# The opening of a hybrid encoder layer: raw x loaded into places of later operands, sums two tiles behind, first outputs inside the first pair

## The chip, the cores and the metric

The kernel runs on one core of a Trainium2 chip. The metric is the time of one execution on the device, in microseconds (us). The engines are PE (TensorE, matrix products), DVE (VectorE), ACT (ScalarE), POOL (GpSimd) and SP (SyncE); here SP's queue issues every DMA. All engines run on their own and wait for each other through semaphores. Each works through its own queue strictly in order, so an instruction that waits holds up all behind it.

## What is computed

The reference is one layer of an encoder: an RMS norm of x (1280 tokens of 2048 channels, 1024 of one sequence and 256 of another), one large projection to 9232 columns, 2-D neighbourhood attention on a part of them, a bidirectional mLSTM on another part, gates, an output projection with the residual, and a last RMS norm.

```python
hn = rmsnorm(x, norm_w)
proj = jnp.einsum('btd,dp->btp', hn, w_in)
...
mixed = jnp.concatenate([att, mem], axis=-1)
return x + jnp.einsum('btm,md->btd', mixed, w_out)
```

Everything is fp32. Only the beginning of the projection matters here.

## The kernel before, in words

**Precision.** A product of fp32 matrices is made from two-part operands: a high part (a cast to fp32r, on ACT) and a low part (the rest, on DVE). Three matmuls replace one: high by high, high by low, low by high (`mm_c`, L186). `split_a` (L157) writes such a pair of parts; `split` (L149) does the same with a scale.

**Stage A of the projection.** The first 768 tokens (GA; two halves of HALF = 384) are projected for all columns, in pairs of 128-column tiles. A pair (`pair_a`, L316) is done in seven products instead of eight: the channels (two halves f of 1024, each of 8 tiles kk) and the tokens (two halves c) form a 2 x 2 block of x, and sums and differences of the blocks are operands of the products. `xop(i, kk, b)` gives operand i: `xb11[kk]` is the upper left block, `xg[0..2, kk]` hold the lower row (products 2 and 3), and two made of sums (6 and 5, 4 and 7). All are kept in SBUF for the whole of stage A. The norm's factor of each token is not applied to x but to the outputs, once it is known.

**The opening.** `first_tiles` (L196) makes these operands and, while that goes on, already computes the first four column tiles in the plain way, with eight accumulators `fb`, one in each PSUM bank. Its loop over kk (0 to 7) does this:
- loads raw x of the tiles kk and kk + 8 (`x_raw`, L107, names `xr`) into buffers of the tag "pc" (NPC = 5 of them), and weights `fr` (L204) into one of NRA = 3 buffers of the tag "ra";
- scales both raw x by the norm's weight (L221, ACT), splits the weights into four `fw` tiles (tag "wsa", NWS = 8), the upper left block into `xb`, the upper right one into `fx` (tag "pc") and the lower row into `xg[0]`;
- 48 matmuls (L188): 24 with the upper row (h = 0) and 24 with the lower row (h = 1);
- four subtractions and additions in place (L241 to L245, DVE), then splits of the results into `xg[1]` and `xg[2]`;
- from kk = 4 on, a load of rows of x (`xq`, L114, tag "ra") and the sum of their squares (`x_square`, L110, ACT).

Eight more squares follow the loop, then the banks are copied out to `fo` (L257 DVE, L259 ACT; tag "pc"), the factor is made of the squares (`x_rstd` L117: a reduction on DVE, L102 and L103 on POOL), spread over the partitions by two small products with six diagonal blocks `xdg` (`x_stats` L123, L131, L134 `rsps`, L135), and the four outputs are scaled by it (`out_scaled`, L161) and written (L265).

**The pairs.** Then come the pairs of the list `order` (L434): A4, A6, A24, A56 and so on; between A6 and A24 stands a small product for the gates (L411). A pair has four stages r, each with one load of 512 KB of weights (L353, tag "ra"), sums of weights on POOL (L358), seven splits (ACT, DVE) and 42 matmuls; in the last stage the products are folded from PSUM into the output tiles `Cn` (tag "pc"). Between products, `next(bg, None)` lets a generator do a piece of background work; after the first pair this is the finishing of the pair before. For the first pair it is empty.

**What sets the order.** The program is not executed in the order of the text. A scheduler orders the instructions of each engine when the kernel is built, and picks for each tile a free buffer of its tag; a load into a buffer waits for the last reader of what lay there. The DMAs also carry eight semaphores in turn, so a DMA waits for the eighth before it.

Of the kernel before, what the change touches and what calls it, by code (L numbers as in the profile page):

```python
# [8 lines left out]
F32 = mybir.dt.float32  # L9
# [21 lines left out]
KC0 = (0, 8, 24, 32)  # L31
BKIND = (0, 1, 1, 2)
BIAS_S = 6 * NAK
XFIRST = (0, 1, 8, 9, 2, 3, 10, 11, 4, 5)
QT0, KT0, GT0, QK0, OT0, ZT0 = 0, 8, 16, 24, 40, 48

# [2 lines left out]
def kernel(  # L39
# [26 lines left out]
    def bank(tag, name):  # L66
        return ps.tile([P, 512], F32, tag=tag, name=name, bufs=3 if tag == "pr" else 5)
# [37 lines left out]
    def x_raw(pool, shape, tag, bufs, g, k):  # L105
        raw = pool.tile([P, shape], F32, tag=tag, name=f"xr{g}_{k}", bufs=bufs)[:, : GSZ[g]]
        DM.dma_start(raw, xT[:, k, GOF[g] : GOF[g] + GSZ[g]])  # L107
        return raw

    def x_square(g, i):  # L110
        t, q = divmod(i, 2)
        r0 = GOF[g] + t * P
        raw = wa.tile([P, 1024], F32, tag="ra", name=f"xq{g}_{i}", bufs=NRA)
        DM.dma_start(raw, xtok[r0 : r0 + P, q * 1024 : (q + 1) * 1024])  # L114
        S.activation(raw, raw, AF.Square, accum_out=ssq[g][:, t, q : q + 1])
# [41 lines left out]
    def split_a(hi, lo, src):  # L157
        S.copy(hi, src)  # L158
        V.tensor_tensor(lo, src, f(hi), op=ALU.subtract)
# [36 lines left out]
    def first_tiles():  # L196
        names = ("pr", "pr", "pr", "a", "a", "a", "a", "a")
        pb = [bank(t, f"fb{j}")[:, :HALF] for j, t in enumerate(names)]
        for kk in range(8):
            wr = wa.tile([P, 1024], F32, tag="ra", name=f"fr{kk}", bufs=NRA)  # L200
            wv = wr.rearrange("p (g j f c) -> p g j f c", g=2, j=2, f=2)
            sc = [x_raw(wa, GA, "pc", NPC, 0, kk)]
# [7 lines left out]
            sc.append(x_raw(wa, GA, "pc", NPC, 0, kk + 8))  # L210
            ws = {}

            def wsplit(h):
                for g_ in range(2):
                    t = wsa(f"fw{kk}_{h}{g_}")
                    hi, lo = (t[:, z].rearrange("p (j c) -> p j c", j=2) for z in range(2))
                    split_a(hi, lo, wv[:, g_, :, h, :])
                    ws[h, g_] = t

            for h in range(2):  # L220
                S.mul(sc[h], sc[h], lnw_sb[:, kk + 8 * h : kk + 8 * h + 1])  # L221
            b11, b12 = sc[0][:, :HALF], sc[0][:, HALF:]
            wsplit(0)
            split_a(xb11[kk][:, 0], xb11[kk][:, 1], b11)
            t12 = wa.tile([P, 2, HALF], F32R, tag="pc", name=f"fx{kk}", bufs=NPC)
            split_a(t12[:, 0], t12[:, 1], b12)
            wsplit(1)
            g0 = xg[0, kk].rearrange("p h c t -> p h (c t)")
            split_a(g0[:, 0], g0[:, 1], sc[1])
            xs = {  # L230
                (0, 0): lambda b_: xb11[kk][:, b_], (0, 1): lambda b_: t12[:, b_],
                (1, 0): lambda b_: xop(2, kk, b_), (1, 1): lambda b_: xop(3, kk, b_),
            }
            for h in range(2):
                for j in range(8):
                    n, c = j // 2, j % 2
                    mm_c(
                        pb[j], lambda a_: ws[h, n // 2][:, a_, (n % 2) * P : (n % 2 + 1) * P],
                        xs[h, c], kk == 0 and h == 0, kk == 7 and h == 1,
                    )  # L240
            V.tensor_tensor(sc[1], sc[1], sc[0], op=ALU.subtract)  # L241
            V.tensor_tensor(b12, b12, b11, op=ALU.subtract)
            d1, t3 = sc[1][:, :HALF], sc[1][:, HALF:]
            V.tensor_tensor(b11, t3, b11, op=ALU.add)
            V.tensor_tensor(d1, d1, t3, op=ALU.subtract)  # L245
            for g_, src in ((1, sc[0]), (2, sc[1])):
                gv = xg[g_, kk].rearrange("p h c t -> p h (c t)")
                split_a(gv[:, 0], gv[:, 1], src)
# [67 lines left out]
    def pair_a(n1, bg=iter(()), hook=None):  # L316
        nm = f"A{n1}"
        tags = ("pr", "pr", "pr", "a", "a", "a", "a")
        order = (1, 5, 6, 4, 7, 2, 3)
        bk = {i: bank(t, f"{nm}b{i}")[:, :HALF] for i, t in zip(order, tags)}  # L320
        Cn = [pc(f"{nm}c{j}") for j in range(2)]
        C = [Cn[q // 2][:, (q % 2) * HALF : (q % 2 + 1) * HALF] for q in range(4)]

        def scaled(q):
            out_scaled(C[q], C[q], rbs[0][:, (q % 2) * HALF : (q % 2 + 1) * HALF], n1)

        def plus(q, src, i):
            V.tensor_tensor(C[q], C[src], bk[i], op=ALU.add)

        def fold(i):  # L330
            if i == 1:
                S.copy(C[0], bk[1])
            elif i == 6:
                plus(1, 0, 6)
            elif i == 7:
                plus(2, 1, 7)
                plus(3, 2, 5)
                plus(1, 1, 5)
                plus(2, 2, 4)
                scaled(3)  # L340
                scaled(2)
            elif i == 2:
                plus(0, 0, 2)
                scaled(0)
            elif i == 3:
                plus(1, 1, 3)
                scaled(1)

        for r in range(4):
            if r == 2 and hook is not None:  # L350
                hook()
            raw = wa.tile([P, 1024], F32, tag="ra", name=f"{nm}r{r}", bufs=NRA)
            DM.dma_start(raw, w_in[n1 // 2, r])  # L353
            A = {(j, f_): raw[:, (2 * j + f_) * 256 :][:, :256] for j in range(2) for f_ in range(2)}

            def summed(i, x, y_, op):
                t = wa.tile([P, 256], F32, tag="wt", name=f"{nm}t{r}{i}", bufs=NWT)
                G.tensor_tensor(t, x, y_, op=op)  # L358
                return t

            src = {1: A[0, 0], 4: A[1, 1], 2: A[0, 1]}
            for i in order:
                if i == 5:
# [15 lines left out]
                if r == 3:  # L379
                    fold(i)  # L380
                elif i in (5, 4, 2):
                    next(bg, None)
        for _ in bg:
            pass
        return finish_a(n1, Cn)
# [1083 lines left out]
```

## Time and profile before

| | us |
|---|---|
| Median of 3 runs (lowest, highest) | 2594.48 (2594.1, 2597.23) |
| The profiled execution | 2593.92 |
| Its span in the profile | 2592.2 |
| PE busy | 2566.7 (99%) |
| DVE busy | 1913.0 (74%) |
| ACT busy | 1310.7 (51%) |
| POOL busy | 559.4 (22%) |

The profile is one execution. Times in its rows are counted from the start of the span. A row of the timeline has start, duration, engine, line, operation, output and input tiles with their form, the number of instructions, and in brackets the idle time before it and what ended that. Two instructions in a row on an engine overlap a little, so that the sum of durations can exceed the time they take together. A row of the waits has the engine, what it was to run, what it waited for, then the sum, the count and the longest. A row of the grouped view has the operation with its form and count, then the sum of the durations and the mean of one in ns, then idle time before them. Matmul records have modelled ends; starts are the better measure.

### The profile page before, as it was taken

How to read it: one execution, taken by the hardware profiler on the slowest of the kernel's cores; microseconds unless marked ns; L12 is line 12 of the kernel's file. 1: busy time of each engine (PE TensorE's matmuls, PEld its weight loads, DVE VectorE, ACT ScalarE, POOL GpSimd, SP SyncE). 2: the span in 40 equal slices, each digit the busy share in tenths (PEclk: the TensorE clock that was granted, in tenths of full speed). 3: DMA queues.
4: the chain of work that ended last, by engine and by line, in shares of the span. 5: the costliest groups of instructions: out<-in, count | busy, mean ns of one | idle time of the engine just before them, and what ended most of it. 6: DMA issues, size and time to landing. Idle time of an engine off the chain costs nothing.

```text
span 2592.2 us, 42374 instructions
## 1 busy us (share of the span) xinstructions
PE 2566.7 (99%) x14470; PEld 2361.1 (91%) x14470; DVE 1913.0 (74%) x3838; ACT 1310.7 (51%) x2988; POOL 559.4 (22%) x857
## 2 busy tenths in 40 slices
PE   8999999999999999999999999999999999999998
PEld 8999999999999999988989989989888888888886
DVE  7858778897878788875487577668567644879695
ACT  7534444444444444543576566567566522335445
POOL 0434444454444444300011010001011000000001
PEclk9999999999999999999999999999999999999999
DMA  6423343333323232445555655655655567646327
GB/s 208 157 78 118 102 135 106 98 102 107 93 96 100 90 116 84 152 127 162 171 171 183 194 155 181 200 169 180 191 183 172 161 231 248 214 127 209 95 86 252
DMA packets 215648, 389.10 MB, mean 150 GB/s; under 512 B 26976, under 2 KB 116232, under 8 KB 215432
## 3 DMA queue, kind: packets, MB, share of 16 engines
q1 hardware_dynamic: 215432, 386.40, 46.7%
q8 instruction: 114, 1.87, 0.3%
q14 instruction: 102, 0.84, 0.1%
HBM read 314.94 MB, written 71.38 MB: 149 GB/s over the span
## 4 chain that ended last, share of the span: by engine, by line
PE 90%; DMA 4%; DVE 2%; ACT 2%; SPq 1%; issue 1%; POOL 0%; ACTq 0%; POOLq 0%; DVEq 0%
PE pc L499 23%; PE po L1303 12%; PE pv L580 6%; PE A24b L188 1%; PE A8b L188 1%; PE A44b L188 1%; PE A40b L188 1%; PE A52b L188 1%; PE A48b L188 1%; PE A20b L188 1%; PE A16b L188 1%; PE A12b L188 1%; PE A54b L188 1%; PE A70b L188 1%; PE A50b L188 1%; PE A68b L188 1%
## 5 line engine op out<-in xcount | busy, mean ns | idle before, releaser
L1303 PE MATMUL po<-wo,mo 128*128 128x512 f32 x1620 | 375.6, 393 | 0.2 <-DVE y L1253 0.2
L1303 PEld LDWEIGHTS po<-wo,mo 128*128 128x128 f32 x1620 | 304.0, 188 | 71.1 <-DVE y L1253 0.7
L152 DVE TENSOR_TENSOR ws<-wr,ws 128x512 fp32r<-128x512 f32 x224 | 152.3, 696 | 96.3 <-ACT ws L151 94.9
L151 ACT CAST ws<-wr 128x512 fp32r<-128x512 f32 x224 | 135.8, 619 | 146.5 <-PE pc L499 101.5
L102 POOL TENSOR_SCALAR rs<-rs 128x1 f32<-128x1 f32 x10 | 3.4, 340 | 541.8 <-DVE rs L1283 541.8
L151 ACT CAST mo<-mb 128x640 fp32r<-128x640 f32 x72 | 51.9, 726 | 108.1 <-PE po L1303 93.6
L152 DVE TENSOR_TENSOR mo<-mb,mo 128x640 fp32r<-128x640 f32 x72 | 58.7, 822 | 33.7 <-ACT mo L151 33.6
L1253 DVE TENSOR_TENSOR y<-y,po 128x512 f32<-128x512 f32 x90 | 58.3, 683 | 9.7 <-PE po L1303 9.4
L152 DVE TENSOR_TENSOR wsv<-wr_v,wsv 128x512 fp32r<-128x512 f32 x64 | 43.6, 690 | 22.1 <-ACT wsv L151 21.8
L151 ACT CAST mo<-ms 128x640 fp32r<-128x640 f32 x40 | 28.9, 726 | 59.9 <-PE po L1303 34.0
L151 ACT CAST wsv<-wr_v 128x512 fp32r<-128x512 f32 x64 | 39.2, 617 | 38.8 <-PE pc L499 23.3
L165 DVE TENSOR_TENSOR pco<-pc,rstdb 128x512 f32<-128x512 f32 x48 | 32.7, 687 | 32.0 <-PE pc L499 29.9
L102 POOL TENSOR_SCALAR mls_0r<-mls_0r 128x2 f32<-128x2 f32 x4 | 0.9, 236 | 245.6 <-ACT mls_0jk L1089 245.6
L274 DVE SCALAR_TENSOR_TENSOR pcv<-pco,cw_sb,pcv 128x516 f32<-128x516 f32 x64 | 46.7, 744 | 0.0
L1266 ACT ACTIVATE jk<-y 128x512 f32<-128x512 f32 x40 | 25.2, 630 | 35.2 <-DVE y L1253 35.0
L152 DVE TENSOR_TENSOR mo<-ms,mo 128x640 fp32r<-128x640 f32 x40 | 32.7, 821 | 7.5 <-ACT mo L151 7.5
L188 PE MATMUL fb<-xg,fw 128*128 128x384 f32 x192 | 35.0, 335 | 1.7 <-ACT xg L158 1.7
L499 PE MATMUL pc<-x_2h,ws 128*128 128x512 f32 x112 | 35.3, 398 | 0.0
L499 PE MATMUL pc<-x_0h,ws 128*128 128x512 f32 x112 | 35.2, 398 | 0.0
L188 PEld LDWEIGHTS fb<-xg,fw 128*128 128x128 f32 x192 | 33.4, 188 | 2.0 <-ACT xg L158 2.0
L499 PE MATMUL pc<-x_1h,ws 128*128 128x512 f32 x112 | 34.5, 395 | 0.0
L499 PE MATMUL pc<-x_8h,ws 128*128 128x512 f32 x112 | 33.9, 396 | 0.0
(1687 smaller groups left out, 8147.9 us busy)
## 6 DMA issues: line engine op xcount, KB each, us to landing
wr<-in_w_in_dram SPq DMA_DIRECT2D x112, 512.0 KB
wr_v<-in_w_in_dram SPq DMA_DIRECT2D x32, 512.0 KB
wb<-in_w_o_dram SPq DMA_DIRECT2D x48, 256.0 KB
xq<-in_xtok_dram SPq DMA_DIRECT2D x20, 512.0 KB
mb<-mx SPq DMA_DIRECT2D x32, 320.0 KB
y<-in_xtok_dram SPq DMA_DIRECT2D x40, 256.0 KB
wr_wp<-in_w_o_dram SPq DMA_DIRECT2D x16, 512.0 KB
xr<-in_xT_dram SPq DMA_DIRECT2D x16, 384.0 KB
```

Of the source, the lines that this page charges most:

```text
L102: G.tensor_scalar(out, ssum, 1.0 / count, EPS, op0=ALU.mult, op1=ALU.add)
L151: S.copy(hi, src)
L152: V.tensor_tensor(lo, src, f(hi), op=ALU.subtract)
L165: V.tensor_tensor(o, src, rb, op=ALU.mult)
L188: PE.matmul(o, w(a_), x(b_), start=first and m == 0, stop=last and m == 2)
L274: V.scalar_tensor_tensor(dst[:, a:n], src[:, a + j - pad : n + j - pad], cw_sb[:, ct, j : j + 1], dst[:, a:n], op0=ALU.mult, op1=ALU.add,)
L499: PE.matmul(pb[j], t[j][:, wi, c : c + P], xs[xi], start=first and m == 0, stop=last and m == 2,)
L580: PE.matmul(outs[tt], xs[:, tt * P : (tt + 1) * P], t[:, wi, q * w : (q + 1) * w], start=first and m == 0 and (gates or tt % 2 == 0), stop ...
L1253: V.tensor_tensor(Y[p, q, tt], Y[p, q, tt], bk, op=op)
L1266: S.activation(jk, Y[p, q, tt], AF.Square, accum_out=ss[t][:, c : c + 1])
L1303: PE.matmul(bk[tt], m[xi][:, tt * P : (tt + 1) * P], w[wi], start=first and kk == 0 and j == 0, stop=last and j == 2, skip_group_check=True,)
```

## The change

- Raw x of kk 0 to 6 no longer goes into the tag "pc". It is loaded into the place of an operand that is made only later: kk 0 to 3 into that of `xg[2, kk + 4]`, kk 4 to 6 into that of `xg[1, kk + 1]`. The operands of `xg` are allocated when first used. Raw x of kk 7 stays in "pc".
- For kk 0 raw x of each half comes in two loads of 384 columns, the first split is made straight from the unscaled raw x (scaling inside the cast and the subtraction), and the products of its 24 matmuls are taken in another order. A multiply of one column of `mhalf` by 1.0 is put ahead of everything on ACT.
- The sums and the splits of the two operands made of them (`sums`) come LAG = 2 channel tiles later. Those of kk 6 and 7, eight of the twelve squares, the factor and the first outputs leave `first_tiles`, which becomes a generator, and are the background work of the first pair.
- In every pair the output tiles `Cn` are taken at stage 3 instead of at the start.

```diff
+LAG = 2
...
+        def ops(g_, kk):
+            if (g_, kk) not in xg:
+                xg[g_, kk] = xa.tile([P, 2, 2, HALF], F32R, tag=f"xg{g_}_{kk}", name=f"xg{g_}_{kk}")
+            return xg[g_, kk]
...
+        def load(kk, h):
+            if kk == 7:
+                r = pc(f"xr{kk}_{h}")
+            elif h == 0:
+                tag = f"xg2_{kk + 4}" if kk < 4 else f"xg1_{kk + 1}"
+                t = xa.tile([P, 2, GA], F32, tag=tag, name=f"xr{kk}")
+                r, raw[kk, 1] = t[:, 0], t[:, 1]
+            else:
+                r = raw[kk, 1]
+            raw[kk, h] = r
+            n = GA if kk else HALF
+            for c in range(0, GA, n):
+                DM.dma_start(r[:, c : c + n], xT[:, kk + 8 * h, c : c + n])
+
+        def scale(kk, h):
+            r = raw[kk, h]
+            n = GA if kk else HALF
+            for c in range(0, GA, n):
+                S.mul(r[:, c : c + n], r[:, c : c + n], lnw_sb[:, kk + 8 * h : kk + 8 * h + 1])
+
+        def sums(kk):
+            r0, r1 = raw[kk, 0], raw[kk, 1]
+            V.tensor_tensor(r1, r1, r0, op=ALU.subtract)
+            V.tensor_tensor(r0[:, HALF:], r0[:, HALF:], r0[:, :HALF], op=ALU.subtract)
+            V.tensor_tensor(r0[:, :HALF], r1[:, HALF:], r0[:, :HALF], op=ALU.add)
+            V.tensor_tensor(r1[:, :HALF], r1[:, :HALF], r1[:, HALF:], op=ALU.subtract)
+            for h in range(2):
+                split_a(slot(1 + h, kk, 0), slot(1 + h, kk, 1), raw[kk, h])
+
+        S.mul(mhalf[:, 15:16], ones[:, 0:1], 1.0)
         for kk in range(8):
...
-            for h in range(2):
-                S.mul(sc[h], sc[h], lnw_sb[:, kk + 8 * h : kk + 8 * h + 1])
...
+            if kk:
+                scale(kk, 0)
+                wsplit(0)
+                split_a(*xb, r0[:, :HALF])
+                split_a(t12[:, 0], t12[:, 1], r0[:, HALF:])
+            else:
+                split(*xb, r0[:, :HALF], lnw_sb[:, 0:1])
+                wsplit(0)
+                split(t12[:, 0], t12[:, 1], r0[:, HALF:], lnw_sb[:, 0:1])
+                scale(kk, 0)
+            scale(kk, 1)
             wsplit(1)
...
-                for j in range(8):
+                for j in (0, 2, 4, 6, 1, 3, 5, 7) if kk == 0 else range(8):
...
-            V.tensor_tensor(sc[1], sc[1], sc[0], op=ALU.subtract)
...
+            if kk >= LAG:
+                sums(kk - LAG)
             if kk > 3:
                 x_square(0, kk - 4)
-        for i in range(4, 12):
-            x_square(0, i)
         Cn = [pc(f"fo{n}") for n in range(4)]
...
+        yield
+        for kk in range(8 - LAG, 8):
+            for i in range(4):
+                x_square(0, 4 * (kk - 8 + LAG) + 4 + i)
+                if i % 2:
+                    yield
+            sums(kk)
+            yield
         x_rstd(0)
         dgt = pc("xdg0")
         x_stats(0, lambda c: dgt[:, c * HALF : (c + 1) * HALF])
+        yield
         for n in range(4):
             out_scaled(Cn[n], Cn[n], rbs[0], n)
             DM.dma_start(pT[n][:, 0:GA], Cn[n])
+            if n % 2:
+                yield
...
     def pair_a(n1, bg=iter(()), hook=None):
...
-        Cn = [pc(f"{nm}c{j}") for j in range(2)]
-        C = [Cn[q // 2][:, (q % 2) * HALF : (q % 2 + 1) * HALF] for q in range(4)]
...
+            if r == 3:
+                Cn += [pc(f"{nm}c{j}") for j in range(2)]
+                C += [Cn[q // 2][:, (q % 2) * HALF : (q % 2 + 1) * HALF] for q in range(4)]
...
-    first_tiles()
+    opening = first_tiles()
+    next(opening)
...
-    bg = iter(())
+    bg = opening
```

More of the change, by code (lines that the diff above doesn't have):

```diff
@@ L198, in first_tiles, with slot @@
         pb = [bank(t, f"fb{j}")[:, :HALF] for j, t in enumerate(names)]
+        raw = {}
+        def ops(g_, kk):
+            if (g_, kk) not in xg:
+                xg[g_, kk] = xa.tile([P, 2, 2, HALF], F32R, tag=f"xg{g_}_{kk}", name=f"xg{g_}_{kk}")
+            return xg[g_, kk]
+        def slot(g_, kk, z):
+            return ops(g_, kk).rearrange("p h c t -> p h (c t)")[:, z]
+        def load(kk, h):
[25 more added lines that the diff above has]
+        S.mul(mhalf[:, 15:16], ones[:, 0:1], 1.0)
         for kk in range(8):
@@ L201, in first_tiles @@
             wv = wr.rearrange("p (g j f c) -> p g j f c", g=2, j=2, f=2)
-            sc = [x_raw(wa, GA, "pc", NPC, 0, kk)]
+            load(kk, 0)
             for g_ in range(2):
@@ L209, in first_tiles @@
                 )
-            sc.append(x_raw(wa, GA, "pc", NPC, 0, kk + 8))
+            load(kk, 1)
             ws = {}
@@ L218, in wsplit @@
                     ws[h, g_] = t
-            for h in range(2):
[L221 to L224, printed above, removed]
-            t12 = wa.tile([P, 2, HALF], F32R, tag="pc", name=f"fx{kk}", bufs=NPC)
-            split_a(t12[:, 0], t12[:, 1], b12)
+            r0 = raw[kk, 0]
+            xb = xb11[kk][:, 0], xb11[kk][:, 1]
+            t12 = wa.tile([P, 2, HALF], F32R, tag="pc", name=f"fx{kk}", bufs=NPC)
+            if kk:
[9 more added lines that the diff above has]
+            scale(kk, 1)
             wsplit(1)
-            g0 = xg[0, kk].rearrange("p h c t -> p h (c t)")
-            split_a(g0[:, 0], g0[:, 1], sc[1])
+            split_a(slot(0, kk, 0), slot(0, kk, 1), raw[kk, 1])
             xs = {
@@ L240, in first_tiles @@
                     )
[L241 to L248, printed above, removed]
+            if kk >= LAG:
+                sums(kk - LAG)
             if kk > 3:
                 x_square(0, kk - 4)
-        for i in range(4, 12):
-            x_square(0, i)
         Cn = [pc(f"fo{n}") for n in range(4)]
@@ L320, in pair_a @@
         bk = {i: bank(t, f"{nm}b{i}")[:, :HALF] for i, t in zip(order, tags)}
-        Cn = [pc(f"{nm}c{j}") for j in range(2)]
-        C = [Cn[q // 2][:, (q % 2) * HALF : (q % 2 + 1) * HALF] for q in range(4)]
+        Cn, C = [], []
         def scaled(q):
```

## The prediction

> **What bounds the kernel now.** First the page: the shares of the engines, and its chain of work that ended last.
>
> ```profile
> PE 2566.7 (99%) x14470; PEld 2361.1 (91%) x14470; DVE 1913.0 (74%) x3838; ACT 1310.7 (51%) x2988; POOL 559.4 (22%) x857
> PE 90%; DMA 4%; DVE 2%; ACT 2%; SPq 1%; issue 1%; POOL 0%; ACTq 0%; POOLq 0%; DVEq 0%
> ```
>
> PE is the bound, so only PE's idle time can be won. The table of windows tells where it is (columns: window, length, busy us and count of PE, PEld, DVE, ACT, POOL, granted clock, DMA share, GB/s), and PE's waits in the first 200 us tell for whom.
>
> ```profile
> 0.00:120.00 120.00, 106.86 (x585) 104.17 (x586) 95.56 (x171) 79.88 (x158) 26.02 (x35) 1.00 0.60 190
> 120.00:400.00 280.00, 280.00 (x1621) 278.55 (x1620) 207.68 (x389) 120.73 (x299) 122.52 (x150) 1.00 0.34 107
> ```
> ```profile
> PE fb L188 <- ACT xb L158: 8.9, 2, 7.9
> PE fb L188 <- ACT xg L158: 1.7, 1, 1.7
> PE A4b L188 <- DVE A4s L159: 1.4, 2, 0.8
> PE A4b L188 <- ACT A4s L158: 1.1, 2, 0.9
> ```
>
> 13.1 of PE's idle us lie in the first 120 us, which the diff rewrites; after that PE is full. In the built program of the changed kernel all five engines' orders equal those of before from early in the second pair (A6) on. So the change is worth what it shifts the start of A6, and I carry that to the end one to one. PE's timeline:
>
> ```profile
> 7.92 0.69 PE L188 MATMUL fb<-xb,fw 128*128 128x384 f32 x1 [7.92 <-ACT xb L158]
> ...
> 15.06 4.32 PE L188 MATMUL fb<-xg,fw 128*128 128x384 f32 x24
> ...
> 68.26 4.43 PE L188 MATMUL fb<-xg,fw 128*128 128x384 f32 x24 [1.68 <-ACT xg L158]
> ...
> 77.38 3.63 PE L188 MATMUL fb<-xg,fw 128*128 128x384 f32 x20
> 81.95 0.61 PE L188 MATMUL A4b<-xb,A4s 128*128 128x384 f32 x2 [0.94 <-ACT A4s L158]
> ...
> 115.03 1.20 PE L188 MATMUL A6b<-xb,A6s 128*128 128x384 f32 x6
> ...
> 144.16 2.95 PE L411 MATMUL gAb<-xb,gAt 128*128 128x384 f32 x16
> ```
>
> The 384 opening matmuls (fb) run from 7.92 to 81.01, the first pair (A4) from there to 115.03. A6 is the undisturbed measure: 168 matmuls in 29.13 us, 0.1734 each. The first 24 fb matmuls took 7.14 instead of 4.16 us (a slow start), two gaps of 1.0 and 1.7 follow, and A4 takes 34.0 where 29.1 and two small products would do.
>
> What makes the gaps stands in the waits of SP and ACT:
>
> ```profile
> SPq L107 <- DVE xg L159: 12.4, 5, 4.8
> ```
> ```profile
> ACT xr L221 <- DMA xr<-in_xT_dram: 7.9, 4, 4.0
> ACT xq L115 <- DMA xq<-in_xtok_dram: 4.8, 4, 2.9
> ```
>
> SP can't load the next raw x until DVE has made the sums out of the old one (five tiles "pc"), so ACT's scaling comes late; and ACT stands before squares whose rows haven't landed.
>
> **Part 1, the first matmul.**
>
> ```profile
> 4.93 1.28 ACT L221 ACT_TABLE_LOAD   x1 [4.93 <-DMA xr<-in_xT_dram]
> 6.22 0.93 ACT L221 ACTIVATE xr<-xr,lnw_sb 128x768 f32<-128x768 f32 x1
> 7.06 0.39 ACT L158 CAST fw<-fr 128x256 fp32r<-128x256 f32 x1
> 7.36 0.51 ACT L158 CAST xb<-xr 128x384 fp32r<-128x384 f32 x1
> ```
> ```profile
> 6.81 7.75 DMA fr<-in_w_in_dram
> ```
>
> The new one-column multiply on mhalf pulls the table load (1.28) ahead of the data, and the first halves are split straight from raw x, so the 0.93 of scaling goes behind them. What is late next is the weight piece fr. No row shows it land. It can't before x has (4.93), and at 7.06 it had: with 0.44 more to the first matmul, that one lies between 5.4 and 7.5 (8.0 if the extra DMA issue costs 0.5). The chain of waits has the third weight tile landed at 14.56; from 4.93 to then 2.75 MB came, 0.286 MB per us, so the first 0.26 MB is there at 5.85. I take **6.3: -1.6 us**, bounds -2.5 and +0.1.
>
> **Part 2, the loop.** The 14 raw halves of kk 0 to 6 now need no free buffer (they lie where operands come later); the built SP order has them all before the first xq. At 0.286 MB per us they and five weights (8.1 MB) are in near 32 us; PE comes to kk 6 at about 59. Only kk 7 waits (two "pc" tiles, freed by kk 2 and 3), and the weight of kk 6 behind it on SP lands near 45, also before 59. Of twelve squares, four stay in the loop. DVE is the tighter cover:
>
> ```profile
> L159 DVE TENSOR_TENSOR xg<-xr,xg 128x768 fp32r<-128x768 f32 x23 | 21.9, 956 | 4.2 <-ACT xg L158 4.0
> L159 DVE TENSOR_TENSOR fw<-fr,fw 128x256 fp32r<-128x256 f32 x32 | 12.8, 421 | 15.5 <-ACT fw L158 15.5
> L241 DVE TENSOR_TENSOR xr<-xr,xr 128x768 f32<-128x768 f32 x8 | 7.6, 955 | 0.1
> L244 DVE TENSOR_TENSOR xr<-xr,xr 128x384 f32<-128x384 f32 x8 | 4.4, 552 | 0.0
> ```
>
> Per kk 3 x 0.96 + 4 x 0.42 + 0.96 + 5 x 0.55 = 8.3 us (less in fact, as starts overlap), against 48 x 0.1734 = 8.32 on PE; but over half of it (the sums and their splits) now trails by two kk, and PE needs those only in A4. So I expect no gap: 24 slow matmuls (7.14) and 360 x 0.1734 = 62.4 from 6.3 on: fb ends at **75.8 instead of 81.0: -5.2**. If this cover fails, the gaps of 2.7 come back.
>
> **Part 3, the first pair.** Eight squares (12 to 4) and the sums of kk 6 and 7 now stand in it, between A4's own splits in ACT's and DVE's orders. Raw weights and xq share three "ra" tiles, so SP's queue becomes a ladder: a load waits for the square of the tile before it.
>
> ```profile
> 54.90 4.10 DMA xq<-in_xtok_dram
> ...
> 76.23 4.34 DMA A4r<-in_w_in_dram
> ```
> ```profile
> 59.07 1.06 ACT L115 ACTIVATE xq<-xq 128x1024 f32<-128x1024 f32 x1 [2.86 <-DMA xq<-in_xtok_dram]
> 60.04 0.19 ACT L115 ACTIVATION_READ_ACCUMULATOR xq<-xq 128x1 f32 x1
> ```
>
> One rung: 4.2 (between the two loads) + 1.2 = 5.4 us. In the built order xq3's square follows a cast that waits for PE to have 108 fb matmuls left: 75.8 - 18.7 = 57.1, so square done 58.6. Then A4's first weights and xq4 load, the second 1.8 behind the first (0.52 MB at 0.286): xq4 squared 65.8, xq5 71.2, xq7 76.6, xq8 82.0, xq10 87.4, and A4's third weight tile (stage 2) lands at **91.6**. Behind xq7 on ACT are the first evacuations of fb's banks, for which A4's second product waits: to 77.35, 0.5 late. Behind xq8 stands stage 1's first cast: ready at 82.3, wanted at 83.6. So PE wants stage 2 at 77.35 - 1.04 + 14.56 = 90.9; its first cast is ready at 92.05. xq9 lands behind xq8 by 82.6, so its follower xq11 is squared at 89.2; after that come reduce, POOL, and DVE's diagonals, ahead of product 5's low part on DVE:
>
> ```profile
> 81.46 0.81 POOL L102 TENSOR_SCALAR rstdc<-rstdc 128x6 f32<-128x6 f32 x1
> ...
> 83.92 2.05 POOL L103 TENSOR_TENSOR rstdc<-rstdc,mhalf 128x6 f32<-128x6 f32 x1
> ```
> ```profile
> 86.00 2.71 DVE L131 TENSOR_SCALAR xdg<-ident,rstdc 128x128 f32<-128x128 f32 x6
> ```
> ```profile
> 87.80 0.88 PE L134 MATMUL rsps<-xdg,ones 128*128 128x384 f32 x2
> 88.22 0.64 PE L188 MATMUL A4b<-xb,A4s 128*128 128x384 f32 x1
> 88.70 0.52 PE L188 MATMUL A4b<-xg,A4s 128*128 128x384 f32 x2
> 89.06 0.81 PE L134 MATMUL rsps<-xdg,ones 128*128 128x384 f32 x2
> 89.41 3.93 PE L188 MATMUL A4b<-xg,A4s 128*128 128x384 f32 x20
> ```
>
> 89.3 + 0.81 + 2.05 = 92.2; POOL's sums for stage 2 stand behind that. Stage 2's first low part is on DVE until 92.45, the diagonals to 95.15, product 5's low part to 95.55. From there 76 matmuls (13.2) and two rsps (0.42 and 0.35 from start to next start): A4 ends at **109.5 instead of 115.0**. The pair itself thus costs 33.7, no better than the 34.0 of before: it trades one set of waits for another. Writing the first outputs falls between stage 3's splits (4 x 1.2 us on DVE), done some 2 us before A6 needs DVE: no cost; without that cover up to 2. A4's own output tiles, now taken only in stage 3, reuse the first outputs' buffers: the first write is issued near 103.5, its reuse comes near 108.4, more than the 4.3 of a load: nothing. A6's fourth weights queue on SP behind these writes, wanted at 131: nothing. The other order of kk 0's products and the three added issues cost PE nothing.
>
> **Sum:** -5.5. The profiled execution took 2593.92 (span 2592.2, 1.7 around it); 2593.92 - 5.5 = 2588.4. The median of the runs is 0.56 above that execution, so **2589.0**.
>
> **The clock.** The first 24 matmuls lost 2.98 us at 0.32 per matmul, and I keep that for the changed kernel; the granted clock in the row of 0 to 120 us reads 1.00 and doesn't show it. The Trainium skill, "TensorE: Matmul & The Clock Gate", section "Part 1: The HAM clock gate", says that PE runs at half clock until one free-running window of about 3.4 us was busy, and again after an idle one. An estimate from that page: by the phase of the window the loss is 1.7 to 3.4, and the sum would be 0.4 worse to 1.3 better.
>
> **The rivals.**
> *No ladder.* If loads take so much less that PE never waits in A4, it ends at 75.8 + 29.1 + 0.8 = 105.7: -9.3, 2585.2. Against: each rung would have to fall well below the 4.1 of a lone load. 5%.
> *The loop still starves.* ACT's order mixes casts of kk with scaling of kk+2, so a late load stops both; gaps of 2.7 return: -2.8, 2591.7. For: DVE near 8.3 per kk. Against: margins of 8 us. 22%.
> *Loads share the engines (the slower side).* Beside every rung another 0.5 MB load is in flight (xq6, the second weights, xq9, xq11, the fourth weights).
>
> ```profile
> 70.00:80.00 10.00, 10.00 (x60) 10.00 (x59) 8.33 (x14) 8.32 (x15) 0.00 (x0) 1.00 0.85 263
> ```
>
> At 263 GB/s that is 2.0 us each; five rungs, each delayed by it, cost 10.0: +4.5, 2599.0, slower than before. It decides from 1.1 us per rung on. Against: DMA is idle most of that time, and the rung's own load is issued first. 8%.
> *PE starts slowly again in A4.* After 7.9 us of idle the first 24 matmuls lost 2.98; after the gap of 1.68 the next 24 took 4.43, nearly the undisturbed 4.16. My longest wait in A4 is 1.8, with 1.2 shortly before it. If that is enough, 3.0 are lost: -2.5, 2592.0. 5%. The Trainium skill, "TensorE: Matmul & The Clock Gate", section "Part 1: The HAM clock gate", puts the fall at an idle window of about 3.4 us; by it my waits would be too short.
> *The change doesn't do what it says* (raw x waits for slots after all): about 0. The built order speaks against it. 3%.
>
> **How the numbers follow.** Forecast 57%, from 2587 to 2590.5 by its terms (first matmul, rungs of 4.10 or 4.34: 5 x 0.24). The range for 8 in 10 takes in the starving loop and the second slow start, not the ends: **2586.3 to 2592.3**. 0.2% is 5.2 us, about what a measurement of this kernel can tell from no change, and the forecast lies just on it: faster by over 0.2% **0.48** (three quarters of the forecast, and no ladder), within 0.2% **0.46**, slower by over 0.2% **0.06** (sharing, worse than priced).
>
> **What would show it.** The first matmul near 6.3 with the table load before 2; no fb gap, fb's end near 76; ACT waits for xq5, xq7, xq8, xq10 after 66 us with loads of about 4.2; a gap of A4 behind DVE's diagonals; A6 starting near 109.5. Wrong if fb has gaps over 0.5, if A6 starts after 112, or if PE has new gaps after A6.

## The result, and the profile after

The changed kernel takes 2588.83 us (median of 10 runs, 2585.87 to 2592.36) beside 2596.24 for the kernel before (10 runs, 2594.1 to 2602.48): ratio 0.9971, 95% interval 0.9961 to 0.9981, or 7.5 us less, between 4.9 and 10.1. The forecast was 2589.0, 5.5 us less. The profiled execution took 2588.44, with a span of 2586.7.

The page's row of the engines and the table of windows for the first 120 us (columns as before):

```profile
PE 2563.3 (99%) x14470; PEld 2360.6 (91%) x14470; DVE 1913.7 (74%) x3838; ACT 1311.1 (51%) x2991; POOL 553.5 (21%) x857
```
```profile
0.00:120.00 120.00, 111.37 (x626) 110.52 (x627) 97.33 (x177) 82.92 (x168) 25.38 (x38) 1.00 0.61 197
```

PE is the bound as before, and in these 120 us it is idle for 8.6 instead of 13.1. PE's waits in the first 200 us (us in total, times, longest), from the table of waits:

```profile
PE fb L189 <- ACT fw L159: 7.1, 1, 7.1
PE A4b L189 <- DVE A4s L160: 1.5, 1, 1.5
```

Of the idle time of before the gaps within fb and the wait at A4's first product are gone; what stays is the wait for the first matmul and one wait in the middle of A4. PE's timeline gives the places (start, length, engine, line, instruction, count, and in brackets the wait before it):

```profile
7.11 1.65 PE L189 MATMUL fb<-xb,fw 128*128 128x384 f32 x4 [7.11 <-ACT fw L159]
...
13.30 4.32 PE L189 MATMUL fb<-xg,fw 128*128 128x384 f32 x24
...
71.62 4.32 PE L189 MATMUL fb<-xg,fw 128*128 128x384 f32 x24
75.78 1.20 PE L189 MATMUL A4b<-xb,A4s 128*128 128x384 f32 x6
...
93.42 0.96 PE L189 MATMUL A4b<-xg,A4s 128*128 128x384 f32 x4 [1.53 <-DVE A4s L160]
94.22 0.81 PE L135 MATMUL rsps<-xdg,ones 128*128 128x384 f32 x2
...
108.02 1.20 PE L189 MATMUL A6b<-xb,A6s 128*128 128x384 f32 x6
```

The first 24 matmuls take from 7.11 to 13.30, the other 360 of fb run without a gap to 75.78 (62.48 us, 0.1736 each), and A6 starts at 108.02 instead of 115.03: 7.0 us earlier. The chain of waits of the same execution (start, length, what; the view leaves out its shorter pieces) shows what A4 hangs on:

```profile
59.24 4.32 DMA xq<-in_xtok_dram
63.71 0.90 issue
64.82 3.66 DMA xq<-in_xtok_dram
68.56 1.15 ACT xq L116 x2
69.74 3.88 DMA xq<-in_xtok_dram
73.99 0.67 issue
74.87 3.65 DMA xq<-in_xtok_dram
78.75 0.82 issue
79.78 3.63 DMA xq<-in_xtok_dram
83.56 0.90 issue
84.66 4.28 DMA A4r<-in_w_in_dram
89.91 3.12 DVE xdg L132 x6
93.42 0.96 PE A4b L189 x4
```

From 59 to 89 us the chain is in the main load, square, load, square: the ladder of the prediction ("issue" in these rows is the time in which a square runs). It ends in A4's third weight tile; then come the diagonals on DVE, and PE's wait.

From A6 on the two executions run alike, but not to the microsecond: the span ends 5.5 us earlier, not 7.0. The rows below put that down to the scatter of one execution: from A6's start to the end of the span 14 profiled executions, of kernels whose changes all lie before or around A4, take between 2475.8 and 2484.8 us (before 2477.2, changed kernel 2478.7 and, a second time, 2478.0). Most of the scatter lies between 1600 and 2000 us, where PE is idle for 2.2 us (before) to 6.9 (start_only). The three executions with the old start have the least idle time there, 2.2 to 2.4 us, and the shortest rest; no run shows whether that is chance. What happens before A6 is therefore read from the traces, and the whole only from the ratios.

### The profile page after: what moved, and what is told of

It is laid out like the page before. It is cut to its first block, busy times and chain, and to the rows that moved or that the text cites. A ratio compares the mean times of both kernels' runs of the same rounds, so it can differ in the third digit from the quotient of the medians.

```text
span 2586.7 us, 42365 instructions
## 1 busy us (share of the span) xinstructions
PE 2563.3 (99%) x14470; PEld 2360.6 (91%) x14470; DVE 1913.7 (74%) x3838; ACT 1311.1 (51%) x2991; POOL 553.5 (21%) x857
## 4 chain that ended last, share of the span: by engine, by line
PE 86%; DMA 5%; DVE 5%; ACT 2%; issue 1%; SPq 0%; POOL 0%; ACTq 0%; POOLq 0%; DVEq 0%
PE pc L552 22%; PE po L1356 12%; PE pv L633 5%; PE A24b L189 1%; PE A8b L189 1%; PE A44b L189 1%; PE A20b L189 1%; PE A16b L189 1%; PE A40b L189 1%; PE A48b L189 1%; PE A52b L189 1%; PE A54b L189 1%; PE A38b L189 1%; PE A50b L189 1%; PE A68b L189 1%; PE A46b L189 1%
## 5 line engine op out<-in xcount | busy, mean ns | idle before, releaser
L153 DVE TENSOR_TENSOR mo<-mb,mo 128x640 fp32r<-128x640 f32 x72 | 58.5, 818 | 32.6 <-ACT mo L152 32.6
L153 DVE TENSOR_TENSOR mo<-ms,mo 128x640 fp32r<-128x640 f32 x40 | 32.6, 818 | 7.3 <-ACT mo L152 7.3
L116 ACT ACTIVATE xq<-xq 128x1024 f32<-128x1024 f32 x20 | 21.2, 1061 | 28.3 <-DMA xq<-in_xtok_dram 28.3
L552 PE MATMUL pc<-x_4h,ws 128*128 128x512 f32 x112 | 33.9, 397 | 0.0
```

The costliest lines, as they stand in the source:

```text
L552: PE.matmul(pb[j], t[j][:, wi, c : c + P], xs[xi], start=first and m == 0, stop=last and m == 2,)
```

## The experiments

All start from the changed kernel. The table holds what was measured. "25th" is the start of the 25th matmul, "A4" and "A6" the start of these pairs on PE, "pair" the time between the two, "rest" the span less A6; the ratio is that of the times to the kernel before, with its interval (diag_act and after_again have one execution each, and no ratio).

| kernel | 25th | A4 | A6 | pair | rest | ratio |
|---|---|---|---|---|---|---|
| before | 15.06 | 81.95 | 115.03 | 33.1 | 2477.2 | 1 |
| changed | 13.30 | 75.78 | 108.02 | 32.2 | 2478.7 | 0.9971 [0.9961, 0.9981] |
| after_again | 12.02 | 74.50 | 110.36 | 35.9 | 2478.0 | |
| start_only | 12.92 | 86.19 | 119.18 | 33.0 | 2484.8 | 1.0006 [0.9996, 1.0015] |
| place_only | 12.51 | 82.34 | 116.21 | 33.9 | 2480.4 | 1.0007 [0.9997, 1.0017] |
| place_lag | 13.39 | 81.95 | 115.91 | 34.0 | 2483.4 | 1.0008 [0.9999, 1.0018] |
| pair_only | 12.87 | 85.62 | 117.77 | 32.2 | 2478.5 | 1.0008 [0.9998, 1.0017] |
| place_pair | 14.33 | 76.89 | 110.40 | 33.5 | 2479.8 | 0.9976 [0.9967, 0.9985] |
| diag_act | 13.76 | 76.29 | 107.83 | 31.5 | 2481.5 | |
| xq_place | 13.01 | 75.49 | 105.96 | 30.5 | 2480.5 | 0.9965 [0.9953, 0.9976] |
| xq_no_preload | 12.37 | 74.85 | 105.32 | 30.5 | 2479.0 | 0.9961 [0.9947, 0.9975] |
| xq_fr_first | 12.31 | 76.32 | 107.01 | 30.7 | 2478.3 | 0.9971 [0.9960, 0.9981] |
| no_start | 14.59 | 78.91 | 112.33 | 33.4 | 2475.8 | 0.9986 [0.9976, 0.9995] |
| xq_no_start | 14.50 | 77.02 | 111.30 | 34.3 | 2476.0 | 0.9976 [0.9966, 0.9985] |

### Which part closes the gaps, and which one pays

The theory at this point: the loop was short of places for raw x, as in the prediction, and the places alone bring about half of the gain. The rival: the trailing sums and the deferred squares relieve DVE and ACT, and that is it. Four kernels take the parts alone.

**start_only**: raw x back in the shared tiles, no lag, squares and outputs before the first pair.

```diff
-LAG = 2
+LAG = 0
...
-            if kk == 7:
-                r = pc(f"xr{kk}_{h}")
-            elif h == 0:
-                tag = f"xg2_{kk + 4}" if kk < 4 else f"xg1_{kk + 1}"
...
+            r = pc(f"xr{kk}_{h}")
...
+        for i in range(4, 12):
+            x_square(0, i)
         Cn = [pc(f"fo{n}") for n in range(4)]
```

> Only the opening's start is new (table load ahead, first halves split from raw x, new order of the first products) and A4's output tiles are taken late; raw x is back in the five shared tiles, sums at once, squares and first outputs before the first pair. Theory (places are what the loop was short of): first matmul at 7.1 and fb 24 matmuls in at 13.3 as in the changed kernel, but loads paced by the five tiles give the 1.7 us back as longer gaps: fb ends between 80 and 81, A6 starts between 114 and 115, time within 1.5 us of before. Rival (what is won at the start is kept): fb ends at 79.3, A6 starts at 113.3.

Measured: ratio 1.0006. The early start is worth nothing in the time, as the theory had it. In the profiled execution the gap it feeds is 5.3 us (PE waits for ACT's split of x), a second wait of 2.5 stands ahead of A4, and A6 starts at 119.18, later than the expected 114 to 115. That execution took 2605.7 us, the longest of the ten (median 2596.53), so these lengths are not typical.

**place_only**: the places stay, lag and deferral go.

```diff
-LAG = 2
+LAG = 0
...
+        for i in range(4, 12):
+            x_square(0, i)
         Cn = [pc(f"fo{n}") for n in range(4)]
```

> New start and new places for raw x; sums are made at once (no lag), squares and first outputs stand before the first pair as in before. Theory: the places alone close the gaps: fb without a gap over 0.3, its end between 75.8 and 76.5; but eight squares stand ahead of A4's first weights on the load queue, some 2 us each after 58.7, so A4 starts near 78.5 and A6 near 111.5: half of the gain of the changed kernel. Rival (lag and deferral relieve DVE and ACT, the places are little): gaps of 1 us or more come back, fb ends after 77.5.

Measured: ratio 1.0007, no gain at all. PE's waits and the load queue (SP) of this execution:

```profile
PE A4b L189 <- ACT A4s L159: 7.2, 1, 7.2
```
```profile
52.13 22.82 SPq L115 DMA_DIRECT2D xq<-in_xtok_dram  x9
76.39 5.01 SPq L399 DMA_DIRECT2D A4r<-in_w_in_dram  x3
```

Half of the theory holds: with the places fb has no gap, without any lag, and ends at 82.34 - 7.19 = 75.2. The other half falls: the nine loads of squares hold SP, A4's first weights are issued only at 76.39, and PE waits 7.2 us for them, where 2.5 had been expected. So in the kernel before two things ended together near 81 us, the starved loop and the chain of squares. Taking one away only shows the other.

**place_lag**: as place_only, with the lag.

```diff
+        for kk in range(8 - LAG, 8):
+            sums(kk)
+        for i in range(4, 12):
+            x_square(0, i)
         Cn = [pc(f"fo{n}") for n in range(4)]
```

> As place_only, but the sums trail by two channel tiles, so those of tiles 6 and 7 stand behind the loop, ahead of the first pair. Theory: the lag is worth nothing in a loop that has no gaps: fb ends between 75.8 and 76.5, A6 starts within 0.7 of place_only or up to 2 later, as the trailing sums (2 x 4.6 us on DVE) now stand ahead of A4's splits. Rival (lag is what closes the gaps): fb ends over 1 us earlier than in place_only.

Measured: ratio 1.0008; A4 waits 5.9 us, A6 starts at 115.91, 0.3 before place_only, and fb (81.95 - 5.91 = 76.0, from a 25th matmul 0.9 later) is as long. The lag closes no gap.

**place_pair**: places and deferral, without the lag.

```diff
-LAG = 2
+LAG = 0
...
-        for kk in range(8 - LAG, 8):
+        for kk in range(2):
             for i in range(4):
-                x_square(0, 4 * (kk - 8 + LAG) + 4 + i)
+                x_square(0, 4 * kk + 4 + i)
                 if i % 2:
                     yield
-            sums(kk)
             yield
```

> As the changed kernel but without the lag: sums at once; eight squares and the first outputs stand in the first pair. Theory: fb ends between 75.8 and 76.5, A4 has the one gap behind the diagonals, A6 starts between 107.7 and 108.6, time as the changed kernel (7 us under before). Rival (DVE's 8.3 us per tile need the lag): gaps over 1 us in fb, A6 after 109.5.

Measured: ratio 0.9976 [0.9967, 0.9985], which can't be told from the changed kernel's. fb has no gap (62.56 us from the 25th matmul), so the rival's reason is out. A6 starts at 110.40, later than expected and where the rival had it; its 25th matmul came 1.0 later than in the changed kernel, and A4's waits (0.38, 0.20 and 1.66) are longer. Whether the lag is worth that microsecond stays open, since the changed kernel itself scatters by more (after_again).

**pair_only**, the fourth corner: deferral without places or lag. Its edit is the `load` of start_only with the LAG of 0 and the loop of squares of place_pair. The theory now reads: two conditions stand one behind the other, and each part takes one away.

> New start, raw x back in the five shared tiles and sums at once, but eight squares and the first outputs in the first pair as in the changed kernel. After place_only (no gap in fb, yet A4 waits 7.2 us for weights behind the squares) and place_pair (A4 starts without a wait) the theory reads: the end of A4 is set by two things one behind the other, and each part of the change takes one away. Then here the gaps of fb stay (fb from the 25th matmul to its end 66 to 73 us instead of 62.5) and A4 starts without a wait and takes 32 to 33.5: A6 starts between 113 and 118, time between 2 under and 4 over before. Rival (the deferral alone is the whole gain, and the places matter as little as place_only suggests): fb takes under 64, A6 starts before 110, time 5 or more under before.

Measured: ratio 1.0008. The gaps of fb are there (4.4 and 1.0), so is one of 1.9 ahead of A4's first product, where the theory had none, and A6 starts at 117.77. PE's rows:

```profile
85.62 1.93 PE L189 MATMUL A4b<-xb,A4s 128*128 128x384 f32 x6 [1.85 <-ACT fo L291]
87.35 7.39 PE L189 MATMUL A4b<-xg,A4s 128*128 128x384 f32 x36
94.57 1.20 PE L189 MATMUL A4b<-xb,A4s 128*128 128x384 f32 x6
```

The pair takes 32.2 us, as expected, but no wait inside it makes it long: the first 42 matmuls take 8.95 us from start to start where the next 42 take 7.28. PE is slow behind the wait (see the last section).

With places and without, with deferral and without, the ratios are 1.0006 (neither), 1.0007, 1.0008 and 0.9976 (both): only both together pay. That is shown by the runs, and it is the main thing that the prediction's sum by parts did not say.

### Is it the ladder that sets A4?

**xq_place**: five of the eight squares load into the two operand places that stay empty until the trailing sums.

```diff
-        raw = wa.tile([P, 1024], F32, tag="ra", name=f"xq{g}_{i}", bufs=NRA)
+        tag = {5: "xg2_6", 7: "xg2_6", 6: "xg2_7", 9: "xg2_7", 11: "xg2_7"}.get(i) if g == 0 else None
+        if tag is None:
+            raw = wa.tile([P, 1024], F32, tag="ra", name=f"xq{g}_{i}", bufs=NRA)
+        else:
+            raw = xa.tile([P, 2 * GA], F32, tag=tag, name=f"xq{g}_{i}")[:, :1024]
```

> The changed kernel, but five of the eight squares in the first pair (5, 6, 7, 9, 11) load their rows into the two operand places of tiles 6 and 7 that stay empty until the trailing sums, so loads of weights and rows no longer wait for the square two before them. Theory (the ladder of three buffers makes the one gap of A4, 1.5 us, since it makes the diagonals late): no gap over 0.3 in A4, which takes 29.9 to 30.6 from its start to A6 instead of 32.2; the time is 1.5 to 2 under the changed kernel, which the runs can't resolve, so the trace decides. Rival (DVE's own work of the pair makes the gap): A4 keeps a gap of 1 us or more behind a DVE split.

Measured: no wait of PE from the first matmul to A6; the pair takes 30.5 us, A6 starts at 105.96, and the time is 0.9965 of before. PE's timeline:

```profile
75.49 1.20 PE L193 MATMUL A4b<-xb,A4s 128*128 128x384 f32 x6
...
105.96 1.20 PE L193 MATMUL A6b<-xb,A6s 128*128 128x384 f32 x6
```

With the same squares on the same engine, but loads that needn't wait for them, the wait is gone. Not only the landing moved: in the built orders squares and diagonals stand earlier too (the diagonals start at 80.55 instead of 89.83). So the run shows what freed loads bring together with the order that follows from them, not the loads in an unchanged order. The other runs point the same way. None of the three further executions with freed loads (xq_no_preload, xq_fr_first, xq_no_start) has a wait of PE behind a DVE split; all four that keep the ladder together with the places and DVE's diagonals have one, of 1.35 to 1.80 us (changed, after_again, place_pair, no_start). 30.47 is also the price of an undisturbed first pair: 168 matmuls at 0.1734 are 29.13, so the four small products of the row sums take 1.34, not the 0.77 of the prediction.

**diag_act**: the diagonals on ACT.

```diff
-                V.tensor_scalar(
-                    dg[:, ts_], ident, rc[:, c * n + t : c * n + t + 1], None, op0=ALU.mult
-                )
+                if g == 0:
+                    S.mul(dg[:, ts_], ident, rc[:, c * n + t : c * n + t + 1])
...
```

> The changed kernel with the six diagonals made by ACT instead of DVE. They took DVE 3.2 us ahead of the low part that PE waited for. Theory (that place in DVE's order is the gap's last cause, behind the ladder): ACT makes them in 6 x 0.2 to 0.3 us, the wait of A4's fifth product falls from 1.5 to between 0.2 and 0.8, as ACT's casts now stand behind them; A4 takes 30.8 to 31.6. Rival (the POOL sums behind the power are the last wait): the gap stays between 1.3 and 1.7.

Measured: the wait is 0.29, now for ACT, and the pair takes 31.5.

```profile
92.34 1.51 PE L192 MATMUL A4b<-xg,A4s 128*128 128x384 f32 x6 [0.29 <-ACT A4s L162]
```

The last link of the wait is thus the place of the diagonals in DVE's order, 3.21 us ahead of a split; the first link is the ladder that makes them, and the weights, so late.

**after_again**: the changed kernel itself, unaltered.

> The changed kernel once more, unaltered, for the scatter of one execution. From the runs so far: first matmul between 6.5 and 7.6, fb from the 25th matmul 62.4 to 62.6, A4 32.0 to 32.6 with the one gap of 1.2 to 1.9, from A6's start to 1115 us within 0.7 of the others, and the rest, in which all runs so far differ by 7 us, anywhere between 1474 and 1482.

Measured: nothing like the 32.0 to 32.6 that was expected of the pair. The 25th matmul and A4 come 1.3 us earlier than in the first execution, and A6 2.3 later:

```profile
74.50 1.20 PE L189 MATMUL A4b<-xb,A4s 128*128 128x384 f32 x6
...
88.90 1.43 PE L189 MATMUL A4b<-xg,A4s 128*128 128x384 f32 x6 [0.70 <-ACT A4s L159]
90.24 1.44 PE L189 MATMUL A4b<-xb,A4s 128*128 128x384 f32 x6
91.73 0.61 PE L189 MATMUL A4b<-xg,A4s 128*128 128x384 f32 x2
94.14 1.29 PE L189 MATMUL A4b<-xg,A4s 128*128 128x384 f32 x4 [1.80 <-DVE A4s L160]
95.22 1.48 PE L135 MATMUL rsps<-xdg,ones 128*128 128x384 f32 x2
95.93 5.60 PE L189 MATMUL A4b<-xg,A4s 128*128 128x384 f32 x24
101.37 0.81 PE L135 MATMUL rsps<-xdg,ones 128*128 128x384 f32 x2
...
103.08 1.21 PE L189 MATMUL A4b<-xb,A4s 128*128 128x384 f32 x6
110.36 1.20 PE L189 MATMUL A6b<-xb,A6s 128*128 128x384 f32 x6
```

ACT's rows show the ladder: its squares start at 68.02, 72.89 and 79.23, where the first execution has 68.56, 73.69 and 78.60; one load came late.

```profile
79.23 1.06 ACT L116 ACTIVATE xq<-xq 128x1024 f32<-128x1024 f32 x1 [3.08 <-DMA xq<-in_xtok_dram]
...
89.78 0.41 ACT L159 CAST A4s<-A4r 128x256 fp32r<-128x256 f32 x1 [0.93 <-DMA A4r<-in_w_in_dram]
```

The third weight tile is cast at 89.78 instead of 89.05 though PE was there earlier, so PE waits longer; and after the second wait it is slow: 24 matmuls from 95.93 take 5.44 to the next row's start at 101.37, where 24 took 4.16 at 71.62 in the first execution. What PE had won at the start it lost, and more. This is the prediction's rival of a second slow start, in an execution of the very kernel that did without it the first time.

### Is the new start worth anything?

**no_start** and **xq_no_start**: the changed kernel and xq_place with the old start.

```diff
-        S.mul(mhalf[:, 15:16], ones[:, 0:1], 1.0)
...
-                for j in (0, 2, 4, 6, 1, 3, 5, 7) if kk == 0 else range(8):
+                for j in range(8):
...
-            if kk:
...
+            scale(kk, 0)
+            scale(kk, 1)
+            wsplit(0)
+            split_a(*xb, r0[:, :HALF])
+            split_a(t12[:, 0], t12[:, 1], r0[:, HALF:])
```

> The changed kernel with the old start: no early table load, the first halves scaled whole and then split, the first products in the old order. Theory (in the changed kernel A4's end is set by the ladder of loads, which hardly moves with PE, so what PE wins at the start it waits for in A4; of the two executions seen, the one whose 25th matmul came 1.3 us earlier had 3.6 us of waits in A4 instead of 1.8): 25th matmul near 15.1 instead of 13.3 and 12.0, fb 62.5 from there, but A4 takes only 30.5 to 31.4 and A6 starts between 108 and 109, as with the new start; time within 1.5 us of the changed kernel. Rival (the start's 1.8 us pass through to the end): A4 takes 32.2 or more, A6 starts at 109.8 or later.

> xq_place with the old start. Theory (once the ladder is broken, PE never waits in A4 and the start's gain passes through): 25th matmul near 15.1, fb 62.5, A4 30.5: A6 starts at 108.0, 2 us later than in xq_place (105.96). Rival (something else behind the ladder, such as the loads themselves, sets A4's end there too): A6 starts within 0.7 of xq_place.

Measured: 0.9986 and 0.9976; A6 at 112.33 and 111.30, later than either theory had it. In no_start the pair (33.4) and A6 fall where the rival had them, in xq_no_start neither side's numbers came. But the runs don't tell the start's worth, for the edit moved more than the start: in ACT's built order a square now stands among the copies that free fb's banks, and A4's products wait for these copies. PE's rows in xq_no_start:

```profile
81.16 7.06 PE L193 MATMUL A4b<-xg,A4s 128*128 128x384 f32 x30 [1.90 <-ACT fo L295]
88.06 1.21 PE L193 MATMUL A4b<-xb,A4s 128*128 128x384 f32 x6
```

This wait and the slow matmuls behind it are the whole of what its pair takes over xq_place's, 34.3 instead of 30.5.

**xq_no_preload**: xq_place without the early table load alone, in which every other instruction keeps its place.

```diff
-        S.mul(mhalf[:, 15:16], ones[:, 0:1], 1.0)
```

> xq_place without the early table load alone; unlike in the two kernels with the old start, the order of all other instructions on every engine is that of xq_place. Theory (with the ladder broken, A4 never waits and A6 follows PE's start one to one): the table load (1.28 us) stands behind the first x half again, first matmul between 7.0 and 8.2, from the 25th matmul to A6 92.9 to 93.2 as in xq_place (92.95), so A6 starts as much later as the 25th matmul does, by 0.3 to 1.5 us. Rival (A4's end is still set by loads): A6 starts within 0.3 of xq_place although the 25th matmul is later, or A4 has a gap of over 0.3.

Measured: ratio 0.9961, the lowest of all, and no wait in A4. From the 25th matmul to A6 it takes 92.95 us as in xq_place (105.32 - 12.37, 105.96 - 13.01): with the ladder broken, A6 follows the start one to one in these two executions. But the first matmul, expected at 7.0 to 8.2, came at 6.64, no later than the 6.89 with the early table load: here that load isn't worth anything. ACT's first rows of xq_place, then of xq_no_preload:

```profile
0.78 1.28 ACT L243 ACT_TABLE_LOAD   x1 [0.78 <-PEq L1511]
...
6.43 0.40 ACT L163 CAST fw<-fr 128x256 fp32r<-128x256 f32 x1 [1.35 <-DMA fr<-in_w_in_dram]
```
```profile
3.88 1.28 ACT L159 ACT_TABLE_LOAD   x1 [3.88 <-DMA xr<-in_xT_dram]
...
6.20 0.39 ACT L163 CAST fw<-fr 128x256 fp32r<-128x256 f32 x1
```

With the early load ACT stands idle for 1.35 us before the cast of the first weight piece; without it, that time covers the table load. In the changed kernel's two executions the same wait is 0.95 and 0.94, so there the 1.28 could be worth some 0.3 us; the first matmul scatters by more (6.44 to 7.55 with the same start).

**xq_fr_first**: the first weight piece ahead of the second half of x.

```diff
             for g_ in range(2):
+                if kk == 0 and g_ == 1:
+                    DM.dma_start(raw[0, 0][:, HALF:], xT[:, 0, HALF:GA])
                 DM.dma_start(
```

> xq_place with the first weight piece issued second on the load queue, ahead of the second half of the first x row (the first matmul waits for the cast of that piece, 2.4 to 3.2 us after the first x half was there). Theory (its turn in the queue is what makes it late): first matmul between 5.8 and 6.4 instead of 6.4 to 7.6, A6 starts between 104.9 and 105.9, time as xq_place or up to 1 us less, 9 to 10 under before. Rival (the landing of a first weight piece takes its time wherever it stands): first matmul between 6.5 and 7.5, A6 as in xq_place.

Measured: the first matmul comes at 5.97, the earliest of all, as the theory had it; the piece's turn in the queue is what it waits for. But ACT's order has moved again: A4's first product waits 1.25 us for a copy of fb, A6 starts at 107.01 instead of the expected 104.9 to 105.9, and the ratio (0.9971) is no better than that of xq_place.

The fastest version tried is xq_place, with or without the early table load: 0.9965 and 0.9961. Its A6 starts 2.1 to 5.0 us before that of the changed kernel's two executions; the ratios' intervals overlap, so in the time this is not settled.

## Why the prediction was right, and where it wasn't

**The sum.** A6 was to start 5.5 us earlier and started 7.0 and, in the second execution, 4.7 us earlier; the time moved by 7.5 [4.9, 10.1]. That the forecast of the time, 2589.0, lies 0.2 us from the measured 2588.83 is luck: it takes 5.5 off the 2594.48 of before, and measured beside the changed kernel the kernel before took 2596.24. That the shift is carried to the end holds as far as the rest's scatter of 9 us lets one see.

**Part 1, -1.6.** The first matmul came at 7.11 and 6.44 instead of 6.3; with this start, in the other kernels, it came between 6.56 and 7.55. The prediction named the weight piece as what is late next but took it to land near 5.9; ACT waited for it until 6.65. The table load, for which the step was argued, was worth nothing in xq_place and at most some 0.3 us here. The slow start cost less than the 2.98 that was kept: the first 24 matmuls took 6.19 and 5.58, a loss of 2.03 and 1.42 (up to 2.87 with the same start, in diag_act). Both errors together left -1.76 at the 25th matmul of the first execution, by luck; in the second it was -3.04.

**Part 2, -5.2 together with part 1.** fb ended at 75.78 where 75.8 was forecast, without a gap, and the rival that the loop still starves is out. But the reason was drawn too wide. The places do it; the lag, to which the prediction gave the cover on DVE, closes no gap (place_only has none without it). And the gain isn't one of this part alone: in place_only fb ends as early and nothing is won. What the loop wins reaches A6 only if the squares no longer stand ahead of A4's weights; the prediction moves them in part 3, but doesn't make that a condition of part 2.

**Part 3, -0.3 more.** The mechanism was right link by link: the ladder, the power on POOL, the diagonals ahead of the fifth product's low part, and a wait behind them. Its size was off. From one square's start to the next on a rung the rows of ACT give 4.92 (63.64 to 68.56), 5.13, 4.91 and 4.89, for 5.4 forecast, since the loads took 3.6 to 3.9 beside the 4.1 and 4.34 taken from before. The third weight tile was in at 88.9 instead of 91.6, POOL's power took 1.38 instead of 2.05, and of the three waits forecast in A4 (0.5, 1.2 and, by what is left of its 33.7, about 2.1, though its text calls 1.8 the longest) one of 1.53 came. Against that the diagonals took 3.21 instead of 2.71 (one of the six takes 0.76 in the median here, beside POOL's sums of weights from 89.74 on, and 0.27 in xq_place, where one such sum runs beside them) and the small products 1.34 instead of 0.77. A4 ended at 108.02, not 109.5.

**The rivals.** The sharing of the DMA engines between loads, the slower side, didn't come: the loads of the ladder were shorter than a lone one of before. "No ladder" is what xq_place makes, and there the pair takes 30.5. The second slow start of PE, given 5%, came in one execution of two; it cost 1.7 us there, not 3.0.

**What the sum by parts hid.** The steps were added along one execution's line of time, and that came out right because all parts were there. Read as the worth of each part, the same numbers mislead: place_only has the new start and the loop's places, for which the sum had 5.2 us, and gains nothing.

## What to carry to other kernels

Where a gap closes, ask what else ends at the same time: before, the starved loop and the chain of squares both ended near 81 us, and neither cure alone moved the time, both together took 6 to 7.5 us. Where loads and the work that frees their buffers take turns, add up the rungs and see whether any idle place can hold one more load; here that took away a wait which a new order of the work (diag_act) only shortened. What one wins ahead of such a ladder may be waited for behind it, as in after_again; the run that was to test this (no_start) moved other work too, so it isn't shown.

## What the runs showed of the hardware

PE falls back to its slow pace after waits shorter than the prediction took for safe. In xq_no_start one wait of 1.90 us is followed by 30 matmuls in 6.90 us (81.16 to 88.06) instead of 5.20, in after_again one of 1.80 by 24 in 5.44 instead of 4.16; after the 1.53 of the first execution the 24 from 94.57 took 4.46 to the next start at 99.03, near the undisturbed 4.16.

The granted clock, read from the table of windows in steps of 0.1 us, says the same. In four executions it falls from 1.00 to 0.50 within 0.5 us of the wait's end, and comes back 3.4 us later: from 81.4 to 84.8 in xq_no_start, 94.6 to 98.0 in after_again, 86.1 to 89.5 in pair_only (after 1.85) and in start_only (after 2.49). Each such stretch costs half of its length, 1.7 us. After waits of 1.53 (changed), 1.66 (place_pair and no_start) and 1.68 (before) it stays at 1.00.

Over the whole span of the 14 executions, past the wait for the first matmul, no wait of PE between 1.2 and 1.7 us is followed by a fall, 9 of the 12 between 1.8 and 3 us are, and so are all four longer ones. Of the three that aren't, one is 2.90 us long (place_lag, at 1785). So the length alone doesn't decide; what else does is not shown. In five executions such a fall comes near 1900 us (start_only, place_only, place_lag, place_pair, diag_act), and they have five of the six longest rests of the table: part of the rest's scatter is this.

At the very start of an execution the clock reads 1.00 although the first matmuls come every 0.32 us; there only the spacing shows the slow pace.

The Trainium skill, "TensorE: Matmul & The Clock Gate", section "Part 1: The HAM clock gate", puts the return to half clock at an idle window of about 3.4 us. These waits disagree, if it is read as a wait of that length; the measurement decides here, and a wait of 1.8 to 1.9 us can be enough.
